# Zero rows for the 64-row products of a hybrid mLSTM, Hyena and neighbourhood-attention trunk

## The chip, the cores and the metric

The kernel runs on one core of one Trainium2 chip. The metric is the device time of one execution in microseconds (us), the median of a few runs. A core has five engines with an instruction queue each: PE (TensorE, matrix products), DVE (VectorE), ACT (ScalarE), POOL (GpSimd) and SP (SyncE, here the issuer of most DMAs). PE multiplies a stationary operand that is loaded into its array first ("PEld" in the profile is that load) with a moving operand that streams through. The array has 128 rows, the contracted dimension, and 128 columns.

## The reference, cut to what matters

Two layers over 1024 latent tokens and 256 context tokens of 1024 channels. The first mixes with an mLSTM and a Hyena long convolution, whose filters come from a small network. The second is a neighbourhood attention of 16 heads of 64 channels; each latent query sees a window of its grid and all context keys. Both layers end in a squared-ReLU MLP.

```python
def hyena_filters(L, w1, b1, w2, b2, w3, freq):
    ...
    h = jnp.sin(freq * (h @ w2 + b2))
    h = (h @ w3).astype(f32).reshape(L, HYENA_ORDER, 2, MIX_B)
    ...
    return h * lax.rsqrt(jnp.sum(h * h, axis=0, keepdims=True) + EPS)

def odd_mixer(hx, hc, w_qkv, qn, kn, rpb, w_out, ctx_out):
    ...
        q = rms_norm(p[:, :, 0], qn) * NA_HD ** -0.5
        k = rms_norm(p[:, :, 1], kn)
    ...
        s_lat = jnp.einsum('bhqd,bhkd->bhqk', q_r, k_blk).astype(f32) + bias.astype(f32)
        s_lat = jnp.where(blk_mask, s_lat, -jnp.inf)
        s_ctx = jnp.einsum('bhqd,bhkd->bhqk', q_r, kc).astype(f32)
        p = jax.nn.softmax(jnp.concatenate([s_lat, s_ctx], axis=-1), axis=-1).astype(v.dtype)
        return (jnp.einsum('bhqk,bhkd->bhqd', p[..., :nk], v_blk)
                + jnp.einsum('bhqk,bhkd->bhqd', p[..., nk:], vc))
```

## The kernel before, in words

Products run in float32r, a float32 whose significand is rounded. To keep accuracy each operand is split into a high part and a low part (the rest after rounding), and a product is the sum hi.hi + hi.lo + lo.hi. Where the contraction has only 64 channels, hi and lo of one operand are stacked on the array's two halves of rows: one product of 128 rows gives hi.hi + hi.lo, and a second one of 64 rows gives lo.hi.

This is done in two stages.

**The filters** (`filter_taps`, early in the program). For each of 8 combinations of channel quarter and order, `w3h` (the high part of the weights, twice, over 128 rows) is multiplied with `h2` (hidden features, hi over lo), then `w3l` (the low part, 64 rows) with the upper half of `h2`: L514 and L515, 6 pairs of products each time, 512 or 256 columns wide. DVE takes the sum out of PSUM, ACT squares it for the norm. Between the pairs on PE stand the products of the filter before (L545 to L549), the transposes of taps (L532) and the sums of the first norm (L253).

**The attention** (`natten_proj`, `natten_attn`). The heads are worked in 8 pairs (`hp`). `natten_proj` computes q, k and v of a pair with `gemm` (L177 to L179), norms q and k (sum of squares by the product L900, then ACT and DVE), and writes q into two tiles Q, one per head hh, with the high part in both halves of the rows (ACT, L930), and the low part into one tile Ql, head 0 in rows 0 to 63, head 1 in rows 64 to 127 (DVE, called from L931, L96 in the profile). The keys go into two tiles KK: k's high part in the head's own half, its low part in the other.

`natten_attn` goes through 4 blocks of columns (cb) and both heads (hh): 8 units a pair of heads, 64 in all. A unit has two row blocks and four pairs of score products: a product with Q over 128 rows (L977), then one with Ql over the 64 rows of its head (L978), 256 columns for the context keys (tile pc) and 384 for the window (tile p_). DVE takes the maximum of the context scores (L981), adds the bias tile TM and takes the maximum of the window scores (L983), ACT forms exponentials (L988, L989), DVE scales them (L993), PE transposes them (L998, L1005), ACT and DVE copy the transposes out (L1000, L1007), and PE multiplies them with the values (L1013, L1017, 64 columns of the array each). The result goes through a tile o to DRAM by a DMA on POOL's queue (L1192). TM is loaded by a DMA on POOL's queue too (L966), and POOL gathers the values' window (L961).

PSUM has 3 banks for scores and results (tag f), 3 for projections (g), one for transposes (m), one for norms (n). A scheduler with priorities sets the order on each engine: the projection of the next pair of heads and the weights' splitting fill the time between the steps of this pair's units. Each engine then works strictly in that order and waits on semaphores.

The functions concerned:

Of the kernel before, what the change touches and what calls it, by code (L numbers as in the profile page):

```python
# [9 lines left out]
F32 = mybir.dt.float32  # L10
F32R = mybir.dt.float32r
# [16 lines left out]
def kernel(ctx: ExitStack, tc: tile.TileContext, A, out):  # L28
# [42 lines left out]
    def psum(**split):  # L71
        """how the eight banks are shared from here on"""
        banks.close()
        psp[:] = [banks.enter_context(tc.tile_pool(name="psp", bufs=1, space=PSUM, reuse_waits="tile")), split]
# [26 lines left out]
    def sub(o, a, b):  # L101
        return tt(o, a, b, ALU.subtract)
# [7 lines left out]
    def split(hi, lo, x, e=None):  # L110
        """x = hi + lo, both rounded to the float32r significand."""
        S.copy(hi, x)  # L112
        (e or V).tensor_tensor(out=lo, in0=x, in1=hi.bitcast(F32), op=ALU.subtract)  # L113

    # ------------------------------------------------------------ constants
# [10 lines left out]
    def rstd_from(ps, n, scale, dst, tmp=None):  # L126
        """dst = (ps * scale + eps) ** -0.5, exp(-0.5 ln v) and one Newton step."""
# [10 lines left out]
    def newton_small(v, dst, tmp):  # L138
        """dst = v ** -0.5 on a small tile."""
# [6 lines left out]
    # ------------------------------------------------------------ weights and products  # L146
# [23 lines left out]
    def gemm(w, h, g, n, M=P, ks=range(8), tag="g"):  # L170
        """out[e, tokens of group g] = sum over the blocks of channels."""
# [25 lines left out]
    # ------------------------------------------------------------ modulation  # L197
# [10 lines left out]
    def mod_steps(l, g, pool, bufs, tag):  # L208
        """2048 columns of the modulation, as 16 steps"""
# [18 lines left out]
    def mod_end(l, g, ps, tag):  # L228
# [9 lines left out]
        # sc1 is blocks 8..15, sc2 blocks 32..39  # L238
# [5 lines left out]
    # ------------------------------------------------------------ norm and modulation of one group of tokens  # L244
    def norm_sum(xk, n, pre, at=None):
        """mean of squares over the channels, in all partitions; xk(k) gives block k"""
# [25 lines left out]
    def norm_group(xk, n, l, sub_i, which, hi, lo, at=None):  # L272
        """xk(k) [P, n] -> hi/lo[:, k, :]"""
# [19 lines left out]
    # ------------------------------------------------------------ MLP  # L293
# [51 lines left out]
    # ------------------------------------------------------------ hyena  # L345
# [10 lines left out]
    def dft_fwd(mm, wp, both=True):  # L356
        """mm(ps, ri, slot) -> X [P, 2, 10, P]"""
# [88 lines left out]
    def sin_reduced(dst, x, pool):  # L446
        """dst = sin(x); x is reduced to [-pi, pi] by a three-part 2 pi."""
# [11 lines left out]
    def filter_hidden(pool, keep):  # L459
        """hidden features, hi over lo; the halves of the positions run in the halves of the partitions"""  # L460
# [37 lines left out]
    def filter_taps(qd, o, h2, dec, fa, fp):  # L498
        """the normed filters of both directions of one channel quarter and order"""
# [3 lines left out]
        w3l = mk(fa, [64, 256], "w3l", 2, F32R)  # L503
# [4 lines left out]
        sub(w3l, w3, w3h[0:64].bitcast(F32))  # L508
        hT = mk(fp, [P, 2, NT], "hT", NHT)
        ss = mk(fp, [P, 4, 2, 3], "ss", 2)  # L510
        for d in range(2):
            for g, (c0, n) in enumerate(GR):
                ps = pt([P, 512], "t")
                T.matmul(ps[:, :n], w3h[:, d * P:(d + 1) * P], h2[:, c0:c0 + n], start=True, stop=False)  # L514
                T.matmul(ps[:, :n], w3l[:, d * P:(d + 1) * P], h2[0:64, c0:c0 + n], start=False, stop=True)  # L515
# [22 lines left out]
    def filter_spectrum(qd, o, hfb, hc, tS, fp, Gd):  # L538
        """spectrum of the two-sided filter -> DRAM"""
# [38 lines left out]
    def hy_block(eb, h, hc, wp):  # L578
        """one block of the projection and its short convolution, [P, 1280]"""
# [29 lines left out]
    def hyena_fft(qd, o, z, hc, wp, Gd):  # L609
        """z (tokens by channels, decimated) -> its product with the filter, ready for the inverse tables"""  # L610
# [16 lines left out]
    def hyena_gate(qd, o, B, X1, x2, hc, wp, mixd):  # L627
        """gate * (filter * z); the last order is left by channels"""
# [24 lines left out]
    # ------------------------------------------------------------ mLSTM  # L653
    def gates(h, mp, keep):
        """gates of all heads as rows 64 d + 10 head + chunk of 128 tokens -> columns, and rows in DRAM to broadcast"""
        with pr("gt"):
            R = 104
            # rows of ps: columns of hi, and of lo 32 below, added up after
# [27 lines left out]
            # lf = min(f, 0) - log1p(exp(-|f|)); log1p(e) = ln(u) + (e - (u - 1)) / u, u = 1 + e  # L686
# [19 lines left out]
            # the running maximum from chunk to chunk: m_prev  # L706
# [49 lines left out]
    def mlstm_head(hd, gs, mp, cst, store):  # L756
        with pr("ms"):
# [36 lines left out]
            # sigmoid(o) = 1 / d, d = 1 + exp(-o): exp(-ln d) and one Newton step  # L794
# [82 lines left out]
    # ------------------------------------------------------------ neighbourhood attention  # L877
# [11 lines left out]
    def natten_proj(hp, h, ap_, nl, cst, order=((0, 0), (0, 1), (1, 0), (1, 1), (1, 2), (2, 0), (2, 1), (2, 2))):  # L889
        """q, k of a pair of heads stacked as hi over lo, and the windows of v"""  # L890
        with pr("np"):
            bd, gain = cst
            # scores = [qhi; qhi] . [khi; klo] + qlo . khi, head hh with khi in its own half
            Q = [mk(nl, [P, LAT], "Q", 4, F32R) for _ in range(2)]
            Ql = mk(nl, [P, LAT], "Ql", 2, F32R)
# [21 lines left out]
            for j, g in order:  # L917
# [5 lines left out]
                if j == 0:  # L923
# [3 lines left out]
                    for hh in range(2):  # L927
# [3 lines left out]
                        sub(blkd(Ql[a, ts]), rv[a], blkd(Q[hh][a, ts]).bitcast(F32))  # L931
# [11 lines left out]
    def natten_attn(hp, qkv, ap_, nl, store):  # L943
        with pr("na"):
# [3 lines left out]
            def tokens(src, n, tag):  # L948
                """channels by tokens -> n blocks of 128 tokens by channels"""
# [8 lines left out]
            for cb in range(4):  # L958
# [5 lines left out]
                for hh in range(2):  # L964
                    TM = mk(nl, [P, 2, 384], "TM", 3)
                    nc.gpsimd.dma_start(TM, A["rpbT"][2 * hp + hh, ct])  # L966
                    a = slice(64 * hh, 64 * hh + 64)
# [4 lines left out]
                    for rb in range(2):  # L972
                        c0 = rb * 512 + cb * P
                        p_ = pt([P, 512], "f")
                        for o, kx in ((pc[:, rb], Kt[hh][:, LAT:NT]),
                                      (p_[:, :384], kl[:, 4 * rb:4 * rb + 12, KC0[cb]:KC0[cb] + 32])):
                            T.matmul(o, Q[hh][:, c0:c0 + P], kx, start=True, stop=False)  # L977
                            T.matmul(o, Ql[a, c0:c0 + P], kx[a], start=False, stop=True)  # L978
# [42 lines left out]
    # ------------------------------------------------------------ layer 0: mixer  # L1021
# [18 lines left out]
    def filler(n, stage):  # L1040
        """n more blocks of q, k, v, o of the heads -> DRAM"""
# [70 lines left out]
    with tc.tile_pool(name="gp", bufs=1, reuse_waits="tile", side="right") as gp:  # L1112
        cst = mlstm_consts(gp)
        with tc.tile_pool(name="ml", bufs=1, reuse_waits="tile") as ml:
# [10 lines left out]
            def out1(d):  # L1125
                """x + gate * product over the first six blocks of the mixer -> DRAM"""
# [56 lines left out]
    # ------------------------------------------------------------ layer 1  # L1183
    with tc.tile_pool(name="nl", bufs=1, reuse_waits="tile") as nl, \
# [3 lines left out]
        def store(hp):  # L1188
            def f(cb, po):
                o = mk(nl, [P, 2, P], "o", 2)  # L1190
# [45 lines left out]
# ---- host side: the inputs laid out for the loads, and constants of the shapes  # L1236
def _layout(I):
    f=lambda a: np.ascontiguousarray(a,dtype=np.float32)
    A={}
    x=np.concatenate([I['x'][0],I['ctx'][0]])          # [1280,1024]  # L1240
# [126 lines left out]
```

## Time and profile before

| | us |
|---|---|
| median of 3 runs (3539.99 to 3546.26) | 3546.22 |
| span of the profiled execution | 3544.9 |
| score products, first to last start (PE) | 2062.0 to 2747.6 |
| w3 products of the filters, first to last start (PE) | 36.3 to 213.9 |
| busy time of POOL | 332.1 |

The span is the time from the first to the last instruction of one execution; the median of the runs stands 1.3 us above it. In the rows of the timeline the shown length of a product includes time in which it is only under way in the array, so what a product costs is the distance from its start to the next one's start. "128*128 128x256" is a product with 128 rows and 128 columns of the array, with a moving operand of 128 partitions and 256 columns; "64*128" has 64 rows. "issue" as the end of an idle time means that nothing which the profile shows was waited for.

### The profile page before, as it was taken

Reading aid. Unit: us, or ns where it says so; the run is one execution under the profiler, and the core shown is the slowest. Engines: PE = TensorE matmul, PEld = TensorE weight load, DVE = VectorE, ACT = ScalarE, POOL = GpSimd, SP = SyncE. Lnnn points to the kernel's source line nnn. Section 1 sums busy time; section 2 is a strip of 40 time slices with the busy share of each in tenths; the row PEclk is TensorE's granted clock in tenths of the full one; section 3 lists DMA queues with packets and bytes.
Section 4 is the critical chain, followed back from the end, with each engine's and each line's share of the span. In section 5 each row is a group of like instructions: output and inputs, shape, how many; then the busy total and the mean of one; then the engine's idle time right before and its main releaser. Section 6 shows DMA issues by size and latency. Waiting matters only on the chain.

```text
span 3544.9 us, 44456 instructions
## 1 busy us (share of the span) xinstructions
PE 3406.1 (96%) x17660; PEld 2676.3 (75%) x17660; DVE 2058.5 (58%) x3655; ACT 1215.0 (34%) x2554; POOL 332.1 (9%) x271
## 2 busy tenths in 40 slices
PE   7889988999989999999999999999999999999999
PEld 3667877677877787787888767777776678888887
DVE  3767979356575444444545875566556665544544
ACT  4643222244343121212121565555555431112211
POOL 0231222101120000000000301111110100000000
PEclk8899999999999999999999999999999999999999
DMA  5331211675632221212110211111113311111111
GB/s 195 133 111 54 85 56 64 230 236 191 209 122 84 75 69 66 77 60 78 48 48 31 79 60 59 60 60 60 60 59 122 106 48 48 48 48 48 48 48 71
DMA packets 104010, 306.06 MB, mean 86 GB/s; under 512 B 12497, under 2 KB 24905, under 8 KB 102394
## 3 DMA queue, kind: packets, MB, share of 16 engines
q1 hardware_dynamic: 94154, 266.60, 22.4%
q0 software_dynamic: 6464, 28.84, 2.6%
q10 hardware_dynamic: 3184, 7.78, 0.7%
q8 instruction: 139, 2.28, 0.3%
q14 instruction: 69, 0.57, 0.0%
HBM read 255.93 MB, written 43.05 MB: 84 GB/s over the span
## 4 chain that ended last, share of the span: by engine, by line
PE 64%; DVE 2%; DMA 2%; ACT 1%; issue 0%; POOL 0%; ACTq 0%; DVEq 0%
PE psg L179 10%; PE psg L177 10%; PE psg L178 10%; PE psf L313 7%; PE psf L314 7%; PE psf L315 7%; PE psf L978 2%; PE psf L977 2%; PE psf L1013 2%; PE psm L218 1%; PE psm L998 1%; PE psn L900 1%; PE psf L1017 1%; DVE n L108 1%; PE psm L1005 1%; DMA wm<-in_w_mod 1%
## 5 line engine op out<-in xcount | busy, mean ns | idle before, releaser
L177 PE MATMUL psg<-h,wh 128*128 128x512 f32 (+1 forms) x2728 | 1020.0, 374 | 17.9 <-ACT wh L112 7.8
L179 PE MATMUL psg<-h,wl 128*128 128x512 f32 (+1 forms) x2728 | 1013.3, 372 | 10.9 <-DVE wl L113 5.9
L178 PE MATMUL psg<-h,wh 128*128 128x512 f32 (+1 forms) x2728 | 1017.5, 373 | 2.4 <-DVE h L108 1.9
L177 PEld LDWEIGHTS psg<-h,wh 128*128 128x128 f32 x2728 | 518.6, 190 | 126.2 <-issue 28.9
L178 PEld LDWEIGHTS psg<-h,wh 128*128 128x128 f32 x2728 | 518.8, 190 | 119.4 <-issue 33.7
L179 PEld LDWEIGHTS psg<-h,wl 128*128 128x128 f32 x2728 | 518.3, 190 | 117.3 <-issue 24.8
L108 DVE SCALAR_TENSOR_TENSOR x<-psf,modT,x 128x512 f32<-128x512 f32 (+1 forms) x512 | 347.2, 683 | 222.6 <-PE psf L315 222.4
L314 PE MATMUL psf<-al,w2h 128*128 128x512 f32 (+1 forms) x1280 | 471.8, 369 | 0.5 <-DVE al L113 0.5
L315 PE MATMUL psf<-ah,w2l 128*128 128x512 f32 (+1 forms) x1280 | 471.3, 368 | 0.0
L313 PE MATMUL psf<-ah,w2h 128*128 128x512 f32 (+1 forms) x1280 | 469.7, 369 | 1.0 <-ACT ah L112 0.8
L112 ACT CAST w2h<-w2r 128x1024 fp32r<-128x1024 f32 x64 | 67.2, 1051 | 762.7 <-PE psf L314 595.9
L313 PEld LDWEIGHTS psf<-ah,w2h 128*128 128x128 f32 x1280 | 240.9, 189 | 45.1 <-ACT ah L112 3.4
L314 PEld LDWEIGHTS psf<-al,w2h 128*128 128x128 f32 x1280 | 241.3, 189 | 42.7 <-DVE al L113 1.8
L315 PEld LDWEIGHTS psf<-ah,w2l 128*128 128x128 f32 x1280 | 241.3, 188 | 41.1 <-issue 1.3
L112 ACT CAST wh<-wr 128x1024 fp32r<-128x1024 f32 (+2 forms) x144 | 148.5, 1031 | 304.0 <-PE psg L178 243.8
L113 DVE TENSOR_TENSOR wl<-wr,wh 128x1024 fp32r<-128x1024 f32 (+1 forms) x105 | 127.7, 1216 | 161.6 <-ACT wh L112 161.6
L108 DVE SCALAR_TENSOR_TENSOR rr<-psg,rr 128x512 f32<-128x512 f32 x160 | 101.4, 634 | 191.7 <-ACT rr L302 191.6
L113 POOL TENSOR_TENSOR wl<-wr,wh 128x1024 fp32r<-128x1024 f32 (+1 forms) x39 | 130.7, 3352 | 622.4 <-ACT wh L112 575.4
L113 DVE TENSOR_TENSOR w2l<-w2r,w2h 128x1024 fp32r<-128x1024 f32 x64 | 78.3, 1223 | 149.2 <-ACT w2h L112 147.5
L302 ACT ACTIVATE rr<-psg 128x512 f32<-128x512 f32 x160 | 88.1, 551 | 213.6 <-PE psg L179 212.3
L112 ACT CAST ah<-rr 128x512 fp32r<-128x512 f32 x160 | 92.4, 578 | 163.6 <-DVE rr L108 163.6
L113 DVE TENSOR_TENSOR al<-rr,ah 128x512 fp32r<-128x512 f32 x160 | 101.8, 636 | 77.6 <-ACT ah L112 77.6
(292 smaller groups left out, 4417.6 us busy)
## 6 DMA issues: line engine op xcount, KB each, us to landing
wm<-in_w_mod SPq DMA_DIRECT2D x96, 512.0 KB
wr<-in_w SPq DMA_DIRECT2D x64, 512.0 KB
w2r<-in_w SPq DMA_DIRECT2D x64, 512.0 KB
big<-d SPq DMA_DIRECT2D x39, 640.0 KB
TM<-in_rpbT POOLq DMA_DIRECT2D x64, 384.0 KB, 3.3
wr<-in_w_in SPq DMA_DIRECT2D x29, 512.0 KB
wr<-in_w_qkv SPq DMA_DIRECT2D x24, 512.0 KB
d<-b SPq DMA_DIRECT2D x8, 1280.0 KB
```

What stands on the lines that cost most here:

```text
L108: return V.scalar_tensor_tensor(out=o, in0=a, scalar=s, in1=b, op0=op0, op1=op1)
L112: S.copy(hi, x)
L113: (e or V).tensor_tensor(out=lo, in0=x, in1=hi.bitcast(F32), op=ALU.subtract)
L177: T.matmul(ps[:M, :n], hi[:, k, :M], hh[g][:, k, :n], start=(i == 0), stop=False)
L178: T.matmul(ps[:M, :n], hi[:, k, :M], hl[g][:, k, :n], start=False, stop=False)
L179: T.matmul(ps[:M, :n], lo[:, k, :M], hh[g][:, k, :n], start=False, stop=(i == len(ks) - 1))
L302: S.activation(r[:, :n], ps[:, :n], AF.Relu)
L313: T.matmul(ps[:, :n], w2h[:, d], ah[g], start=(i == 0), stop=False)
L314: T.matmul(ps[:, :n], w2h[:, d], al[g], start=False, stop=False)
L315: T.matmul(ps[:, :n], w2l[:, d], ah[g], start=False, stop=(i == 1))
L977: T.matmul(o, Q[hh][:, c0:c0 + P], kx, start=True, stop=False)
L978: T.matmul(o, Ql[a, c0:c0 + P], kx[a], start=False, stop=True)
```

## The change

The low parts get as many rows as the array has, with zeros in the added ones. `w3l` becomes 128 rows, with POOL setting rows 64 to 127 to zero before DVE writes the others. Ql becomes one tile per head: the head's low part stands in its own half of the rows, and POOL sets the other half to zero. The products with them (L515, L978; in the changed program L516 and L980) then use all rows of `h2` and KK, and the zeros meet the low parts of the other operand. The memory for it comes from fewer buffers: Ql has 3 of 4 KB per partition for two tiles a pair (before: 2 for one tile), TM 2 of 3 KB in place of 3, o 1 of 1 KB in place of 2.

```diff
         w3h = mk(fa, [P, 256], "w3h", 2, F32R)
-        w3l = mk(fa, [64, 256], "w3l", 2, F32R)
+        w3l = mk(fa, [P, 256], "w3l", 2, F32R)
+        G.memset(w3l[64:128].bitcast(F32), 0.0)
...
-        sub(w3l, w3, w3h[0:64].bitcast(F32))
+        sub(w3l[0:64], w3, w3h[0:64].bitcast(F32))
...
-                T.matmul(ps[:, :n], w3l[:, d * P:(d + 1) * P], h2[0:64, c0:c0 + n], start=False, stop=True)
+                T.matmul(ps[:, :n], w3l[:, d * P:(d + 1) * P], h2[:, c0:c0 + n], start=False, stop=True)
...
-            Ql = mk(nl, [P, LAT], "Ql", 2, F32R)
+            Ql = [mk(nl, [P, LAT], "Ql", 3, F32R) for _ in range(2)]
+            for hh in range(2):
+                G.memset(Ql[hh][64 - 64 * hh:128 - 64 * hh].bitcast(F32), 0.0)
...
-                        sub(blkd(Ql[a, ts]), rv[a], blkd(Q[hh][a, ts]).bitcast(F32))
+                        sub(blkd(Ql[hh][a, ts]), rv[a], blkd(Q[hh][a, ts]).bitcast(F32))
...
-                    TM = mk(nl, [P, 2, 384], "TM", 3)
+                    TM = mk(nl, [P, 2, 384], "TM", 2)
...
-                            T.matmul(o, Ql[a, c0:c0 + P], kx[a], start=False, stop=True)
+                            T.matmul(o, Ql[hh][:, c0:c0 + P], kx, start=False, stop=True)
...
-                o = mk(nl, [P, 2, P], "o", 2)
+                o = mk(nl, [P, 2, P], "o", 1)
```

The rest of the text's difference is comments. Outside the attention the order on PE, DVE and ACT is the same but for single products; POOL has the zeroings between its steps. Three places in the attention show what moves. The names are those of the kernel with a running number behind them; in the changed program every line of `natten_attn` from L969 on stands two lower down than before (L977 is L979), and L900 is L903.

PE, the scores of the last unit of the second pair of heads, before:

```order
L977 MATMUL psf_17260<-KK_16504,Q_16501 128x256
L978 MATMUL psf_17260<-KK_16504,Ql_16502 128x256
L977 MATMUL psf_17262<-KK_16504,Q_16501 128x384
L978 MATMUL psf_17262<-KK_16504,Ql_16502 128x384
L977 MATMUL psf_17260<-KK_16504,Q_16501 128x256
L978 MATMUL psf_17260<-KK_16504,Ql_16502 128x256
L900 MATMUL psn_17462<-n_3105_17460,bd_8236 128x512
L977 MATMUL psf_17268<-KK_16504,Q_16501 128x384
L978 MATMUL psf_17268<-KK_16504,Ql_16502 128x384
```

and the same unit in the changed program:

```order
L979 MATMUL psf_17274<-KK_16518,Q_16512 128x256
L980 MATMUL psf_17274<-KK_16518,Ql_16514 128x256
L979 MATMUL psf_17276<-KK_16518,Q_16512 128x384
L980 MATMUL psf_17276<-KK_16518,Ql_16514 128x384
L979 MATMUL psf_17274<-KK_16518,Q_16512 128x256
L980 MATMUL psf_17274<-KK_16518,Ql_16514 128x256
L903 MATMUL psn_17479<-n_3108_17477,bd_8244 128x512
L177 MATMUL psg_17494<-h_1652_8689,wh_17448 128x512
L178 MATMUL psg_17494<-h_1653_8690,wh_17448 128x512
L979 MATMUL psf_17282<-KK_16518,Q_16512 128x384
L980 MATMUL psf_17282<-KK_16518,Ql_16514 128x384
```

The pairs and the norm product between them keep their places; two projection products have moved up between the last two pairs. The shapes shown are those of the results; the rows of the array are not in them.

DVE, where it writes the low part of q of the third pair of heads, first group of tokens, before:

```order
L96 TENSOR_TENSOR Ql_17331<-n_3095_17371,Q_17329 64x512
L993 TENSOR_SCALAR pe_17013<-pe_17013,st_17007 128x640
L993 TENSOR_SCALAR pe_17019<-pe_17019,st_17007 128x640
L983 ISA pe_17099,st_17087<-psf_17094,TM_17084,st_17087 128x384
L983 ISA st_17087 128x1
L96 TENSOR_TENSOR Ql_17331<-n_3095_17371,Q_17330 64x512
L985 TENSOR_SCALAR st_17087<-st_17087 128x2
```

In the changed program the first head's subtraction stands at the same place, the second head's (into Ql_17346) 32 rows later:

```order
L1009 COPY pc_17190<-psm_17185 128x512
L985 ISA pe_17240,st_17228<-psf_17235,TM_17225,st_17228 128x384
L985 ISA st_17228 128x1
L96 TENSOR_TENSOR Ql_17346<-n_3098_17388,Q_17344 64x512
L987 TENSOR_SCALAR st_17228<-st_17228 128x2
L108 SCALAR_TENSOR_TENSOR n_3103_17432<-psg_17402,gain_8248,n_3103_17432 128x512
```

It has moved to the last block of columns of the second pair, just behind the last scores (psf_17235) of that pair's first head, and ahead of L987 of the same unit.

POOL in the changed program, over the last two blocks of columns of the second pair (zeroings are new, the other steps are those of before with the loads of TM spread out more):

```order
L969 DMA TM_17225<-in_rpbT 128x768
L1194 DMA d_89<-o_17086 256x1x128
L964 COPY vs_17216<-vT_16519 128x512
L969 DMA TM_17272<-in_rpbT 128x768
L898 MEMSET Ql_17346 64x1024
L969 DMA TM_17676<-in_rpbT 128x768
L1194 DMA d_89<-o_17213 256x1x128
L898 MEMSET Ql_18177 64x1024
L969 DMA TM_17723<-in_rpbT 128x768
L1194 DMA d_89<-o_17340 256x1x128
```

Ql_17346 takes the buffer that the second pair's first head still uses, so its zeroing waits for that head's last product with Ql; the loads of TM and the stores of o stand behind it.

More of the change, by code (lines that the diff above doesn't have):

```diff
@@ L964, in natten_attn @@
                 for hh in range(2):
-                    TM = mk(nl, [P, 2, 384], "TM", 3)
+                    TM = mk(nl, [P, 2, 384], "TM", 2)
                     nc.gpsimd.dma_start(TM, A["rpbT"][2 * hp + hh, ct])
-                    a = slice(64 * hh, 64 * hh + 64)
                     kl = Kt[hh][:, 0:LAT].rearrange("p (r c) -> p r c", c=64)
```

## The prediction, made before the changed kernel was run

> **What bounds the kernel now.** I read the page first, for the busy shares and the chain that ended last, then the attention stage by stretches, then who waits for whom there.
>
> ```profile
> PE 3406.1 (96%) x17660; PEld 2676.3 (75%) x17660; DVE 2058.5 (58%) x3655; ACT 1215.0 (34%) x2554; POOL 332.1 (9%) x271
> PE 64%; DVE 2%; DMA 2%; ACT 1%; issue 0%; POOL 0%; ACTq 0%; DVEq 0%
> ```
>
> PE is busy for 96% of the span and nearly all of the chain. The chain's shares add up to 69%, so it is followed back only to about 1100 us: the attention is on it, the filters at the start of the program are not, and for them a stretch has to do. An average over the whole program says little about two small stages, so here are the place of the attention, one stretch inside each stage, and the longest wait of DVE in the attention:
>
> ```profile
> L977 PE MATMUL psf<-KK,Q x256: 276/384/741, 2062.0 to 2747.6; 128*128 128x256 f32 x91, 128*128 128x384 f32 x37
> ...
> core 0: us, PE busy (x) PEld busy (x) DVE busy (x) ACT busy (x) POOL busy (x), PEclk, DMA share, GB/s
> 111.00:122.00 11.00, 11.00 (x66) 8.13 (x65) 10.06 (x21) 7.56 (x18) 2.51 (x3) 1.00 0.55 199
> 2324.00:2411.00 87.00, 86.97 (x514) 61.97 (x513) 52.31 (x115) 51.71 (x129) 9.91 (x16) 1.00 0.19 61
> ...
> DVE st L981 <- PE psf L978: 107.0, 64, 4.1
> ```
>
> The score products run from 2062 to 2748 us. There PE never rests, at the full clock (1.00), while DVE and ACT work 60% of the time, and DVE's first step on each unit (a head and a block of columns, 64 in all) waits 107 us in total for the Ql product. So time taken off PE there comes off the span, until a chain through DVE and ACT becomes the bound. In the filters DVE has 10.06 of 11 us: less room.
>
> But a busy PE is not a PE that computes. The start-to-start distances in the timeline of PE tell what a product really costs (columns: start, shown length, engine, line, operation):
>
> ```profile
> 2357.90 0.28 PE L977 MATMUL psf<-KK,Q 128*128 128x256 f32 x1
> 2358.11 0.38 PE L978 MATMUL psf<-KK,Ql 64*128 64x256 f32 x1
> 2358.42 0.39 PE L977 MATMUL psf<-KK,Q 128*128 128x256 f32 x1
> 2358.65 0.49 PE L998 MATMUL psm<-ident,pe 128*128 128x128 f32 x3
> ...
> 2210.51 0.28 PE L178 MATMUL psg<-h,wh 128*128 128x256 f32 x1
> 2210.63 0.28 PE L179 MATMUL psg<-h,wl 128*128 128x256 f32 x1
> ...
> 2200.47 0.44 PE L978 MATMUL psf<-KK,Ql 64*128 64x384 f32 x1
> 2200.84 0.38 PE L977 MATMUL psf<-KK,Q 128*128 128x256 f32 x1
> ...
> 2203.07 0.50 PE L179 MATMUL psg<-h,wl 128*128 128x512 f32 x1
> 2203.40 0.40 PE L177 MATMUL psg<-h,wh 128*128 128x512 f32 x1
> 2203.64 0.39 PE L178 MATMUL psg<-h,wh 128*128 128x512 f32 x1
> ```
>
> In a stream of full-row products 256 columns take 0.12 us (2210.51 to 2210.63) and 512 take 0.23 (2203.40 to 2203.64). The same 256 columns take 0.21 when the next product has 64 rows (2357.90), 0.23 when the one before had 64 rows (2358.42), and 0.31 for the 64-row product between two others (2358.11). So a change of shape costs about 0.09 us before it and 0.10 to 0.11 after it. The second part shows again at 2203.07: the first full product after an Ql product takes 0.33 in place of 0.23. The weight loads say why:
>
> ```profile
> 2203.06 0.19 PEld L179 LDWEIGHTS psg<-h,wl 128*128 128x128 f32 x1 [0.19 <-issue]
> 2203.17 0.19 PEld L177 LDWEIGHTS psg<-h,wh 128*128 128x128 f32 x1
> 2203.41 0.19 PEld L178 LDWEIGHTS psg<-h,wh 128*128 128x128 f32 x1
> ```
>
> In the stream a load starts a whole product ahead (2203.41 for the product of 2203.64). After the change of shape the load of L179 starts only with its product (2203.06 and 2203.07), after an idle 0.19: its time is not hidden, and before it the array seems to empty, 0.09. The price of a change is 0.19 us. 384 columns fit: 0.37 from 2200.47 to 2200.84, where a value between 0.12 and 0.23 would be 0.175.
>
> **The change, part by part.** How often this is paid:
>
> ```profile
> L978 PE MATMUL psf<-KK,Ql 64*128 64x384 f32 x128 | 57.1, 446 | 0.0
> L978 PE MATMUL psf<-KK,Ql 64*128 64x256 f32 x128 | 48.9, 382 | 0.0
> L515 PE MATMUL pst<-h2s,w3l 64*128 64x512 f32 x32 | 17.7, 553 | 0.0
> L515 PE MATMUL pst<-h2s,w3l 64*128 64x256 f32 x16 | 6.7, 420 | 0.0
> ...
> 111.20 0.47 PE L514 MATMUL pst<-h2s,w3h 128*128 128x512 f32 x1
> 111.61 0.50 PE L515 MATMUL pst<-h2s,w3l 64*128 64x512 f32 x1
> 112.03 0.49 PE L545 MATMUL psf<-hfb,tF 128*128 128x128 f32 x2
> ```
>
> 256 Ql products and 48 w3l products, hardly ever two in a row, make two changes each. Along PE's order 598 changes fall away: 506 in the attention (a few edges stay, where a score product meets the 64-column products L1013 and L1017) and 92 in the filters. The changes to and from 64 and 32 columns stay. The same number of products and columns is left, and a full-row product of the same width costs no more than its columns, as the stream shows. Gross: 506 x 0.193 = 97.7 us, and 92 x 0.19 = 17.5 us (L515 takes 0.42 at 111.61, 0.19 over 0.23).
>
> What of it is kept? Unit 27 of the attention, with the rows that gate PE:
>
> ```profile
> 2345.31 0.69 DVE L981 TENSOR_REDUCE st<-psf 128x2 f32<-128x512 f32 x1 [4.07 <-PE psf L978]
> 2347.45 1.01 DVE L993 TENSOR_SCALAR pe<-pe,st 128x640 f32<-128x640 f32 x2
> 2348.38 0.17 DVE L985 TENSOR_SCALAR st<-st 128x2 f32<-128x2 f32 x1
> ...
> 2348.54 0.49 PE L998 MATMUL psm<-ident,pe 128*128 128x128 f32 x3
> 2350.03 0.49 PE L998 MATMUL psm<-ident,pe 128*128 128x128 f32 x3
> ...
> 2348.59 0.62 ACT L988 ACTIVATE pe<-pe,st 128x384 f32<-128x384 f32 x1
> 2349.20 0.46 ACT L1000 COPY s<-psm 128x384 f32<-128x384 f32 x1
> ```
>
> The transposes L998 at 2348.54 need the first half of L993, done at about 2347.95: 0.6 us of slack. A unit has four pairs of score products, 8 changes, 1.54 us, so PE would wait 1 us per unit if DVE stood still. It doesn't: it had idled 4.07 us for PE's L978 when it began at 2345.31, and its steps follow PE forward. Where they don't follow quite: the second transposes (2350.03) need the one bank of tag m back, copied out by L1000, which stands on ACT behind L988, which waits for DVE's L985; slack 2350.03 - 2349.66 = 0.37. Moving these rows forward by hand I get a wait of about 0.25 us in every second unit: 64 x 0.13 = 8 us, an estimate.
>
> The zeroing of Ql is new on POOL. Two rows of its kind, and the load whose buffers shrink:
>
> ```profile
> masks.py:197 POOL MEMSET ident<- 128x128 f32 x1 | 0.2, 205 | 0.3 <-POOLq L1359 0.3
> L1359 POOL MEMSET const-float32-1.0<- 128x1 f32 x1 | 0.1, 104 | 0.0
> ...
> TM<-in_rpbT POOLq DMA_DIRECT2D x64, 384.0 KB, 3.3
> ```
>
> 104 ns for one column and 205 for 128 make 0.8 ns a column: about 0.9 us for 1024 (1.6 if it is all in proportion), an estimate. 16 of them are 15 us on an engine that is 9% busy. Their price is a wait. With three buffers for two tiles a pair, the second head's Ql lies where the running pair's first head has its own, so its zeroing waits for that head's last scores; behind it DVE's subtraction into that Ql waits, and behind that in DVE's order L985 (now L987) of the same unit, its exponentials, and the r tile, one of four n2 buffers, that the next K norm needs. The zeroing runs while DVE does that unit's last 0.6 us step, so DVE loses about 0.3 us, plus 0.69 for a subtraction that now stands ahead of L985. For 7 pairs between 0 and 11 us; I take 6. Queued behind the zeroing on POOL are the next TM loads and stores of o, which have time: a TM is needed two units (some 20 us) after its buffer is free, and takes 0.6 to issue and 3.3 to land; the single o is needed once per block of columns, again some 20 us apart. I cost both at nothing; if that cover failed, it would be 3 us in some unit. The eight zeroings of w3l, 64x256, are 0.3 us each on an idle POOL, their buffers two filters old: nothing. ACT, SP and the stages after attention keep their work.
>
> Attention: 97.7 - 8 - 6 = 84. Filters: bounds are 0 and 17.5; since DVE is nearly full beside PE there, I keep 60%, 10.5. Together 94. The profiled execution has 3544.9, which becomes 3451; the median of the runs shown is 1.3 above its span, so **3452 us**.
>
> **Rivals.** (1) The chain through DVE and ACT takes over. For: slack is only 0.37 to 0.6 us per unit against 1.54 saved; if DVE stood still, 0.6 of 1.54 would be kept, 38 + 6 us, 3502. Against: DVE's 107 us of waiting for L978. With half kept, 49 + 9: 3488. (2) A load into rows that the running product uses is not hidden, so full-row pairs pay 0.10 for each load and save only the emptying: 598 x 0.09 = 54, 3492 before any wait. Against: the load at 2203.41 lies whole under the product of 2203.40. [...] (3) Slower: the late second Ql holds back the next pair's K norms, and with them its first scores, past the products that fill. The chain of waits shows one group of K in the first pair, from its square to its last step:
>
> ```profile
> 2048.44 0.61 ACT n L898
> ...
> 2059.38 0.70 DVE KK L96
> ```
>
> 11.6 us with other steps between. If one group lay bare in each of 7 pairs, 81 us would go, 3533; two groups make 163, 3615. It decides from 94 / 7 = 13.5 us a pair. Against: PE's new order has those scores in the old place, with 30 and more projection products behind them to fill.
>
> (4) The zero rows change nothing, because what costs is the change of operands and not of rows: 3546 to 3552. Against: the 2203.40 stream changes operands each time.
>
> **How the numbers follow.** Forecast 0.70, with its own range 3430 to 3475; more than gross 0.03; rival 1 0.15; 2 0.05; 4 0.03; 3 0.04. Low end: all 115 us kept, 3431, rounded to 3428; the high end takes in rival 1 at half and the lower edge of 2, 3492. Faster by over 0.2% (7 us, about what a measurement of this kernel tells from no change) 0.93, within 0.03, slower 0.04.
>
> **What would show it.** Right: L980 (before L978) with 128 rows, 0.12 and about 0.175 us to the next start, no "issue" idle before its load; the stretch from the first score product to the last in some 600 us where it has 686; DVE's wait for the scores smaller. Wrong: distances still 0.31 and 0.37 (rival 4), 0.22 and 0.28 (rival 2); PE idle before L1000, L979 or L1015 of over 5 us per pair, released by DVE or ACT (rival 1); idle PE with DVE waiting on POOL's zeroing (rival 3).

## The result and the profile after

The changed kernel takes **3438.66 us** (median of 4 runs, 3435.15 to 3440.34), the kernel before beside it 3543.65 us (4 runs, 3539.99 to 3546.26): a ratio of **0.9706**, 95% interval 0.9692 to 0.9719. That is 105.0 us less; 94 had been forecast, and the time is 13 us below the 3452 on record. The profiled execution spans 3438.5 us.

The page of the changed kernel: busy time and share of each engine, then the shares of the chain that ended last.

```profile
PE 3288.0 (96%) x17660; PEld 2647.1 (77%) x17660; DVE 2055.2 (60%) x3655; ACT 1209.4 (35%) x2554; POOL 350.3 (10%) x295
PE 76%; DVE 12%; DMA 5%; ACT 3%; POOL 3%; issue 2%; SPq 0%; ACTq 0%; DVEq 0%; POOLq 0%
```

PE has as many products as before and 118 us less busy time (3406.1 before). It still bounds the kernel; DVE and ACT are within 6 us of before, and POOL has 18 us more, its zeroings.

The timeline of PE and of the weight loads, in a unit of the attention (start, shown length, engine, line, operation; L979 and L980 are L977 and L978 of before):

```profile
2185.82 0.34 PE L979 MATMUL psf<-KK,Q 128*128 128x384 f32 x1
2186.00 0.34 PE L980 MATMUL psf<-KK,Ql 128*128 128x384 f32 x1
2186.18 0.28 PE L979 MATMUL psf<-KK,Q 128*128 128x256 f32 x1
2186.29 0.28 PE L980 MATMUL psf<-KK,Ql 128*128 128x256 f32 x1
2186.41 0.34 PE L979 MATMUL psf<-KK,Q 128*128 128x384 f32 x1
...
2186.18 0.19 PEld L980 LDWEIGHTS psf<-KK,Ql 128*128 128x128 f32 x1
2186.30 0.19 PEld L979 LDWEIGHTS psf<-KK,Q 128*128 128x128 f32 x1
```

From 2186.00 to 2186.18 a Ql product of 384 columns takes 0.18 (0.37 before), from 2186.29 to 2186.41 one of 256 takes 0.12 (0.31 before). The load for the product of 2186.29 starts at 2186.18, with the product ahead of it. The whole stage, and the filters, by stretches (us, then the busy time of each engine, the granted clock, the DMA share and GB/s), first of the changed kernel and then of the kernel before:

```profile
30.00:250.00 220.00, 182.68 (x1124) 144.09 (x1123) 147.83 (x315) 136.90 (x302) 67.51 (x63) 0.94 0.42 144
2037.00:2641.00 604.00, 593.13 (x3965) 464.94 (x3963) 419.24 (x954) 395.67 (x998) 87.39 (x133) 0.99 0.25 77
```

```profile
30.00:250.00 220.00, 188.52 (x1005) 137.78 (x1006) 145.95 (x308) 128.85 (x286) 55.77 (x49) 0.86 0.39 133
2061.00:2748.00 687.00, 683.70 (x3966) 484.31 (x3965) 419.71 (x954) 399.73 (x999) 75.68 (x119) 0.99 0.21 68
```

In the attention the same work of DVE and ACT (419 and 396 us) stands in 604 us where it had 687, and PE's idle time there has grown from 3.3 us (687 - 683.70) to 10.9. In the filters the granted clock is 0.94 where the profile of before had 0.86. That was not foreseen, and it is what the experiments have to settle.

The place of the changed kernel's score products and of its w3 products, with their first and last start:

```profile
L979 PE MATMUL psf<-KK,Q x256: 274/342/582, 2037.7 to 2640.9; 128*128 128x256 f32 x92, 128*128 128x384 f32 x36
L516 PE MATMUL pst<-h2s,w3l x48: 277/393/430, 39.4 to 190.0; 128*128 128x512 f32 x32, 128*128 128x256 f32 x16
```

And its waits in the attention (us in total, times, longest):

```profile
DVE st L983 <- PE psf L980: 62.3, 40, 2.8
PE psm L1000 <- ACT s L1002: 4.2, 11, 0.8
PE psm L1000 <- DVE pe L995: 2.1, 7, 0.6
...
PE psf L979 <- DVE KK L96: 0.2, 1, 0.2
```

From first to last score product: 603.2 us, 82.4 less than before. DVE's wait for the Ql product has shrunk from 107.0 to 62.3 us, so it still mostly waits for PE, and PE waits for it and for ACT only now and then, at the transposes L1000. Ahead of the attention 24 us have gone too, in the filters; behind it nothing has changed (797.3 us from the last score product to the end before, 797.6 after).

### The profile page after: what moved, and what is told of

Same layout as the page of the kernel before. It is cut to its first block, busy times and chain, and to the rows that moved or that the text cites. A ratio compares the mean times of both kernels' runs of the same rounds, so it can differ in the third digit from the quotient of the medians.

```text
span 3438.5 us, 44541 instructions
## 1 busy us (share of the span) xinstructions
PE 3288.0 (96%) x17660; PEld 2647.1 (77%) x17660; DVE 2055.2 (60%) x3655; ACT 1209.4 (35%) x2554; POOL 350.3 (10%) x295
## 4 chain that ended last, share of the span: by engine, by line
PE 76%; DVE 12%; DMA 5%; ACT 3%; POOL 3%; issue 2%; SPq 0%; ACTq 0%; DVEq 0%; POOLq 0%
PE psg L178 12%; PE psg L179 12%; PE psg L177 12%; PE psf L313 7%; PE psf L314 7%; PE psf L315 7%; DMA wm<-in_w_mod 2%; DVE b L96 2%; PE psf L1015 2%; DVE n L108 2%; PE psm L1000 1%; DVE q L96 1%; PE psm L218 1%; PE psf L979 1%; PE psf L980 1%
## 5 line engine op out<-in xcount | busy, mean ns | idle before, releaser
L178 PE MATMUL psg<-h,wh 128*128 128x512 f32 (+1 forms) x2728 | 1017.1, 373 | 4.1 <-DVE h L108 2.8
L178 PEld LDWEIGHTS psg<-h,wh 128*128 128x128 f32 x2728 | 519.7, 191 | 120.6 <-issue 33.8
```

Of the source, the lines that this page charges most:

```text
L178: T.matmul(ps[:M, :n], hi[:, k, :M], hl[g][:, k, :n], start=False, stop=False)
```

## The experiments

Two questions: is it the change of shape that cost the time, and not another part of the edit; and why did the filters give 24 us in the profile, more than the 17.5 that the prediction had as their most? The comparisons with before are with the runs of the kernel before on the same chip.

**The filter part alone.**

```diff
-        w3l = mk(fa, [64, 256], "w3l", 2, F32R)
+        w3l = mk(fa, [P, 256], "w3l", 2, F32R)
+        G.memset(w3l[64:128].bitcast(F32), 0.0)
...
-                T.matmul(..., h2[0:64, c0:c0 + n], start=False, stop=True)
+                T.matmul(..., h2[:, c0:c0 + n], start=False, stop=True)
```

> The kernel before with the filter part of the change alone: w3l with 128 rows, the lower half of the rows zeroed by POOL, its product over all rows. Theory A (a change between 64 and 128 rows costs about 0.19 us, 92 of them fall away, and what goes beyond that in the profile of the changed kernel came from a higher granted clock by chance): 10 to 17.5 us less, ratio 0.995 to 0.997, and in the stretch from 30 to 250 us the granted clock is 0.86 as in the profile of before. Theory B (the gain is 25 us because PE, less interrupted in the filters, also gets a higher clock): 22 to 26 us less, ratio 0.9927 to 0.9938, granted clock 0.94 in that stretch. The attention takes 685 to 687 us from its first to its last score product by either.

Measured: 3525.68 us against 3541.42, ratio 0.9946 (0.9929 to 0.9963). In its profile the filters' stretch looks as in the changed kernel:

```profile
30.00:250.00 220.00, 181.75 (x1121) 143.31 (x1120) 148.77 (x315) 136.73 (x303) 66.56 (x63) 0.94 0.41 142
```

By its interval that is 13 to 25 us: nearer to theory A in time, with theory B in the clock of its one profile. So this run alone doesn't decide; the clock of one execution is only that of one execution. The attention shows the same. Its code is that of before, and 685 to 687 us were expected, but in this profile it takes 696:

```profile
2033.50:2729.40 695.90, 692.59 (x3961) 489.96 (x3961) 418.20 (x953) 398.95 (x996) 75.49 (x119) 0.98 0.21 67
```

PE works as before; the trace's clock records have three stretches of half clock between 2198 and 2486 us, 24 us together, that the profile of before doesn't have. So the lengths of a stage in two profiles tell two programs apart only where the clocks agree.

**The attention part alone**, with the fewer buffers, filters as before.

> The kernel before with the attention part alone: one Ql tile per head with zeros in the other half of the rows, and the fewer buffers for TM and o; the filters as before. By the theory that 506 changes of shape at 0.193 us fall away and some 15 us of that are lost in waits: 80 to 84 us less, about 3461 us, and the distance from the first to the last score product 603 us. If the filters' shorter time had helped the attention or the other way round, the two parts would not add up to the 105 us of the whole change: then 70 or 95. Granted clock from 30 to 250 us: 0.86 if it belongs to the filters' old products, anything if it is chance.

Measured: 3446.24 us against 3541.42, ratio 0.9722 (0.9699 to 0.9745), so 95 less. The place of its first product of each pair of scores (L978 in this kernel):

```profile
L978 PE MATMUL psf<-KK,Q x256: 274/342/582, 2048.7 to 2652.1; 128*128 128x256 f32 x92, 128*128 128x384 f32 x36
```

and its filters' stretch:

```profile
30.00:250.00 220.00, 189.80 (x1045) 139.48 (x1046) 147.58 (x310) 132.87 (x292) 61.70 (x56) 0.91 0.41 142
```

The stage is 603.4 us long, as expected, but the time fell by 11 us more than the 80 to 84 expected. By the medians alone this would be the outcome "95", in which the two parts don't add up: 16 and 95 are more than 105. The clocks decide that below. The old filters have a clock of 0.91 here and 0.86 in the profile of before: the clock of this stage differs from execution to execution of the same code.

**64 rows kept, the order changed.** In each row block the two Q products come first, then the two Ql products.

```diff
-                        for o, kx in (...):
+                        for o, kx in two:
                             T.matmul(o, Q[hh][:, c0:c0 + P], kx, start=True, stop=False)
+                        for o, kx in two:
                             T.matmul(o, Ql[a, c0:c0 + P], kx[a], start=False, stop=True)
```

> The kernel before with all products, tiles and rows as they were, but in another order: in each row block the two Q products first, then the two Ql products of 64 rows. Half of the 506 changes between 64 and 128 rows in the attention go, nothing else. Theory A (the change of shape is what costs, 0.19 us a time): 49 us less gross, 35 to 45 kept, 3499 to 3509 us; the first of two neighbouring Ql products is 0.12 us (256 columns) from the second less the 0.09 for emptying, that is it still pays on its own edge, and the second pays no load. Rival (a product of 64 rows is itself slow, whatever stands beside it): within 5 us of before. Rival (a weight load into rows that the running product uses can't be hidden): little gain as well, since two Ql products of one head use the same rows.

Measured: 3524.55 us against 3541.42, ratio 0.9945 (0.9922 to 0.9968); 674.7 us from the first to the last score product (685.6 before). The expectation had the number of changes wrong: the scheduler took most of the groups apart again. In the trace only 26 of 128 row blocks have their two Ql products side by side, and 459 changes of rows are left of 511. The 52 that went are worth 52 x 0.193 = 10 us, and the stage is 10.9 shorter, at the same clock (0.99) as before. Where the group held, its timeline prices both edges of a product apart (here L978 is Q and L980 Ql; "x2" is two products in one row, 0.23 apart for Q and 0.22 for Ql):

```profile
2202.70 0.56 PE L978 MATMUL psf<-KK,Q 128*128 128x256 f32 x2
2203.20 0.56 PE L980 MATMUL psf<-KK,Ql 64*128 64x256 f32 x2
2203.69 0.50 PE L178 MATMUL psg<-h,wh 128*128 128x512 f32 x1
...
2202.70 0.30 PEld L978 LDWEIGHTS psf<-KK,Q 128*128 128x128 f32 x2 [0.20 <-issue]
2203.19 0.29 PEld L980 LDWEIGHTS psf<-KK,Ql 64*128 64x128 f32 x2 [0.20 <-issue]
```

Q and Ql of 256 and 384 columns take 0.50 and 0.49 us together (2202.70 to 2203.20 to 2203.69), where their columns are worth 0.12 + 0.175 = 0.295: each group of two pays 0.20, once, whatever its rows. By the trace's starts the first product of a group pays 0.10 (median of 26: 0.223 for a 256-column Ql with another shape ahead of it and the same behind it), the last pays 0.09 (0.268 for a 384-column Ql with the same shape ahead of it and another behind), and a Ql product with other shapes on both sides pays both (0.310 and 0.372). The changed kernel's trace shows the same edges on products of 128 rows: where the 64-column products stand next to a Ql product, it takes 0.223 for 256 columns (6 of them, another shape ahead) and 0.273 for 384 (8, another shape behind). A product of 64 rows is not slow in itself: both rivals of this experiment fall.

**Fewer buffers alone**: TM 2 in place of 3, o 1 in place of 2, all else as before.

> The kernel before with only two buffers for TM in place of three and one for o in place of two; products, Ql and rows as before. Prediction's step: costs nothing, within 3 us (ratio 0.9992 to 1.0008). Rival (part of the 15 us lost in the attention is a TM load or a store of o that comes late): 3 to 10 us more, with DVE's window step waiting for the TM load, or ACT's copy into o for the store before.

Measured: 3539.46 us against 3541.42, ratio 0.9991 (0.9976 to 1.0005); the attention's stretch 687.2 us (685.6). They cost nothing that can be seen, and in the trace DVE has no wait for a TM load, nor ACT one for a store of o.

**The changed kernel again, and the clock.**

> The changed kernel itself, more often, beside runs of the kernel before on the same chip. The two parts alone, taken at equal clock, gave 12 and 84 us of gain, 96 together; the medians differ by 105. Theory A (the 10 us between are a granted clock that happened to be low in the runs of before): with more runs the mean clocks of the two kernels come together, 0.982 to 0.983 each, and the ratio goes to 0.9730. Theory B (the changed kernel is throttled less): mean clock 0.985 against 0.982 again, ratio 0.970 to 0.971.

> The changed kernel beside the two others, for the comparison on the same chip: 3434 to 3442 us, 603 us from the first to the last score product, and a mean clock of 0.984 to 0.986 against 0.982 to 0.984 for the kernel before if it is throttled less, the same clock if not.

Measured: 3436.84 against 3535.97 us (0.9717, 0.9704 to 0.9731) on the one chip, 3433.02 against 3540.95 (0.9702, 0.9680 to 0.9723) on the other; the stretch of scores 603.1 and 600.9 us. On the first chip the ratio lies between the two theories, and the mean clocks are 0.985 and 0.984; on the second they are 0.986 and 0.983. Each run gives its mean granted clock; only all runs together decide:

| | runs | mean us | mean clock | us at a clock of 0.983 |
|---|---|---|---|---|
| before (beside the experiments) | 42 | 3539.2 | 0.9825 | 3538.0 |
| filter part alone | 6 | 3525.0 | 0.9833 | 3525.9 |
| grouped, 64 rows | 5 | 3523.4 | 0.9840 | 3526.1 |
| fewer buffers | 12 | 3538.9 | 0.9827 | 3538.2 |
| attention part alone | 4 | 3447.3 | 0.9852 | 3453.5 |
| changed | 13 | 3436.1 | 0.9854 | 3442.7 |

The last column moves each run along a line fitted through the 42 runs of before, whose time falls by 27.7 us for each 0.01 of clock; the line explains 64% of their variance. At equal clock the filter part is worth 12.1 us, the attention part 84.5, together 96.6, and the whole change 95.3, so the parts add up. The other 8 of the 103 us between the means go with the clock, which is higher by 0.0029 in the changed kernel (standard errors 0.0003 and 0.0004). So theory B holds over all runs: the changed kernel is throttled less, by little.

The filters by themselves say the same. From the first w3 product to the same later product of PE (the 1076th) the four profiles with the old filters take 218.8, 209.9, 209.7 and 205.7 us at clocks of 0.87, 0.93, 0.92 and 0.96 of that stretch; those of the changed kernel and of the filter part alone 192.1, 193.5, 200.6 and 197.1 at 0.95, 0.95, 0.91 and 0.93. At 0.92 to 0.93 that is 209.8 against 197.1, 13 us. A line through all thirteen profiles, with the clock of this stretch and the kind of filters as its two terms, gives 13.4 us (standard error 0.6). The profile of before had the lowest clock of all, and the 9 us by which it lies above 209.8 stood in the first comparison.

**Ql zeroed once.** Before the loop over the pairs, fixed tiles are set to zero; in the loop there is no zeroing. First with one tile for head 1 and two for head 0, then the other way round (diff against the changed kernel; the tiles QL are made ahead of the loop):

```diff
-            Ql = [mk(nl, [P, LAT], "Ql", 3, F32R) for _ in range(2)]
-            for hh in range(2):
-                G.memset(Ql[hh][64 - 64 * hh:128 - 64 * hh].bitcast(F32), 0.0)
+            Ql = [QL[0][hp % 2], QL[1][hp % 1]]
```

> The changed kernel, but the zeros are written once ahead of the loop and not for each pair: head 0 has two tiles of its own for Ql, head 1 one. No zeroing stands in the loop, but the low part of head 1 must wait until the running pair's head 1 has had its last scores, one unit later than in the changed kernel. Theory A (lateness of the second Ql is what costs, the zeroing is hidden): 3 to 10 us more than the changed kernel, with DVE's subtraction waiting longer for the score products. Theory B (the zeroing in the loop costs, 7 times about 0.95 us): 0 to 5 us less. If neither lies on the path: within 3 us.

> The changed kernel, zeros written once ahead of the loop: head 0 has one tile for Ql, head 1 two. The low part waits for the last scores of the running pair's head 0 as in the changed kernel, without the zeroing between. Theory A (lateness): within 2 us of the changed kernel. Theory B (the zeroing in the loop costs 7 times about 0.95 us): 4 to 7 us less. The prediction took 6 us for both together.

> The kernel whose zeros are written once, head 0 with one tile for Ql and head 1 with two, more often. If taking the zeroing out of the loop is a real gain: 3 to 6 us less than the changed kernel on the same chip, and the stretch from the first to the last score product 599 us against 603. If the first difference was noise: within 2 us, and 603 us.

Measured: with one tile for head 1 3440.13 us, ratio to before 0.9728 (0.9713 to 0.9742), 604.6 us for the stretch of scores; with one tile for head 0 3432.44 us, 0.9708 (0.9694 to 0.9721), and again 3430.48 us, 0.9693 (0.9673 to 0.9714), with 599.0 and 598.9 us for the stretch. The changed kernel on the same two chips: 3436.84 and 3433.02 us, 603.1 and 600.9 (the 600.9 at a clock of 1.00, the others at 0.99). In the trace of the changed kernel the zeroing and, with one tile for head 1, DVE's subtraction wait for the score products:

```profile
L898 POOL MEMSET Ql<- 64x1024 f32 x16 | 15.2, 948 | 67.4 <-PE psf L980 67.3
```

```profile
DVE Ql L96 <- PE psf L979: 6.2, 7, 2.3
```

With one tile for head 0 neither wait is there. PE's waits at the transposes, 6.3 us in the changed kernel (4.2 + 2.1), are 2.6 us in it (its L999 is the changed kernel's L1000):

```profile
PE psm L999 <- ACT s L1001: 2.1, 4, 0.7
PE psm L999 <- DVE pe L994: 0.5, 2, 0.3
```

This version is the fastest of all, by 4.2 us in the mean of 9 runs against 13 of the changed kernel (3431.9 against 3436.1), 5.3 at equal clock. On the one chip it came out as theory B had it (4.4 us less), on the other between the two outcomes (2.5 less; 3 to 6 or at most 2 had been expected), with the 599 us of a real gain in both profiles. How the 5 us come about is not shown. In the changed kernel POOL waits 67 us for the score products, but no row has DVE or PE waiting for the zeroing; what moves with the edit is the order of DVE's steps. The version with one tile for head 1 saves the zeroing as well and gains nothing: its median is 3.3 us above the changed kernel, which is not clear of noise, and its stretch of scores is 5.6 us longer than with one tile for head 0. So the subtraction one unit later may well cost that much, but order and wait are not told apart.

**Another bank for the second transposes.** The bank of tag m, which the prediction blamed for 8 us, gets relief: the second transposes of a unit go to tag g (projections), or to tag n (norms).

```diff
-    TA, TB, TC, TV, PO = "m", "m", "m", "m", "f"
+    TA, TB, TC, TV, PO = "m", "g", "m", "m", "f"
```

> The changed kernel, with the second transposes of the window's weights of each unit in a bank of the projections (tag g) in place of the one bank of tag m. Theory A (the 8 us booked for waits behind the transposes come from that one bank, given back by ACT's copy): the waits of the transposes for ACT's copy (4.2 us on PE, 19.9 us of the weight loads) mostly go, 3 to 8 us less than the changed kernel. Rival (ACT and DVE are late anyway, and the wait only moves to the next transposes, or the projections miss the bank): within 2 us or more than the changed kernel, with waits of the projection products for a bank of tag g.

> The changed kernel, with the second transposes of the window's weights in the bank of the norms (tag n), which the projections don't use. In PE's order the projection products stay spread over the units of a pair (30, 4, 14, 2, 5, 2, 5, 2 groups of three) but for the first pair, whose last four units get none. Theory A (the transposes' waits for ACT's copy come from the one bank of tag m): these waits go, 3 to 8 us less in pairs 2 to 8, and some 5 us more in the first pair, together -3 to +2. Theory B (ACT and DVE are late themselves): the wait moves to DVE's scaling of the weights, 0 to 5 us more in pairs 2 to 8, 5 to 10 us more together.

Measured: 3640.68 us with g, ratio to before 1.0288 (1.0271 to 1.0305); 3526.2 us with n, 0.9960 (0.9943 to 0.9977): 204 and 93 us more than the changed kernel on the same chip, far beyond what any theory had put a number to. The stretch of scores, with g and then with n:

```profile
2034.60:2819.70 785.10, 670.64 (x3922) 510.52 (x3922) 418.79 (x944) 400.50 (x994) 84.59 (x133) 0.90 0.18 58
2033.20:2728.50 695.30, 627.66 (x3964) 482.11 (x3964) 425.81 (x951) 401.13 (x996) 85.16 (x133) 0.96 0.21 67
```

With g, two neighbouring stretches of the attention: the first two rows have all work (busy time and count of PE, PEld, DVE, ACT and POOL, then the granted clock, the DMA share and GB/s), the other two the projection products L178 alone (PE and PEld):

```profile
2254.00:2310.00 56.00, 45.11 (x283) 33.47 (x285) 25.42 (x68) 22.61 (x69) 8.26 (x13) 0.73 0.17 56
2310.00:2374.00 64.00, 57.80 (x318) 45.05 (x315) 35.48 (x71) 35.06 (x76) 5.62 (x9) 1.00 0.15 48
...
2254.00:2310.00 56.00, 0.80 (x1) 0.29 (x1) 0.73 0.17 56
2310.00:2374.00 64.00, 24.16 (x63) 11.88 (x63) 1.00 0.15 48
```

The scheduler now puts 63 of the L178 products into one stretch and 1 into another (56 and 50 in the changed kernel in the same stretches). Without them the chain through DVE and ACT lies bare: PE is idle 11 of 56 us, and its clock falls to 0.73. Of the 182 us by which the stage is longer, the clock of 0.90 in place of 0.99 is worth at most 0.09 x 785 = 71, an estimate. With n the order changes too. PE now waits for DVE's scaling of the weights at the transposes, for the last steps of the norms ahead of projections, and for ACT's squares ahead of the norm products L903:

```profile
PE psm L1000 <- DVE pe L995: 19.2, 16, 3.0
PE psg L177 <- DVE n L96: 14.5, 7, 2.1
PE psn L903 <- ACT n L901: 13.2, 19, 1.2
```

The wait of L1000 for L1002 is gone there, and dearer ones stand in its place. Whether the one bank cost the changed kernel anything could not be tried without such side effects, and stays open, and no row names the bank of tag n as what is waited for. Shown is that with this scheduler a bank taken from g or n costs far more than 8 us.

## Why the prediction was right, and where it was off

- **PE bounds, and the change of shape is the price**: right. The distances went from 0.31 and 0.37 to 0.12 and 0.18, and the third experiment showed the two parts, 0.10 on the first product behind a change and 0.09 on the last ahead of one, with the rows kept. Where the 0.10 is paid, the loads of a group start only with its first product (2203.19 and 2203.20), after an idle 0.20, so its load isn't hidden. That the array empties ahead of a change, as the prediction read the other 0.09, was not shown; the rows give the time alone.
- **Attention, 97.7 gross, 84 kept**: 82.4 in the profile and 84.5 at equal clock, but its parts were each too large, and that the two errors cancel is luck. PE's idle time grew by 7.6 us, not by 14; so the changes were worth 82.4 + 7.6 = 90 us, 0.178 each over 506, not 0.193. By the distances from start to start without idle time, 82 of the 90 lie on the score products and 7 on the projection products beside them; why the average is below the 0.19 of the products shown isn't settled.
- **8 us behind the transposes**: the waits of L1000 for ACT and DVE are 6.3 us (4.2 + 2.1), and 1.1 of them stood there before. **6 us for the second Ql**: some 5, by the version without the zeroing in the loop. The size is near, the way is not: the prediction had DVE wait behind the zeroing, and the trace has no such wait. Nor do the two add up, since that version takes away 3.7 of the 6.3 us.
- **Filters, 10.5 of 17.5 kept**: 12.1 by the part alone and 13 by the stages at like clock. The share of 60% was chosen and not worked out, and what takes the other 4 to 5 us isn't shown. Of the 24 us in the first comparison of profiles some 13 are the change, and most of the rest is the low clock in the profile of before.
- **Fewer buffers, zeroing of w3l, POOL's time**: nothing, as booked. A zeroing of 64x1024 took 948 ns where 0.9 us was estimated, of 64x256 307 ns where 0.3 was.
- **The rivals.** (1) DVE and ACT as the bound: DVE still waits 62.3 us for the Ql product, and PE for the transposes in 18 places only. The slack was small for a DVE that stands still, and DVE followed. With the projections bunched the bare chain and the lower clock there (0.90 in the stage) cost 204 us. (2) Loads not hidden: the load at 2186.18 lies beside the product of 2186.18, rows 0 to 127 both, and the distances are 0.12 and 0.18, not 0.22 and 0.28. (3) K norms held back: PE waits once, 0.2 us, for a KK tile. (4) Zero rows change nothing: 82 us.

The step that was off is one that the prediction didn't write as a term: it subtracted 94 us from the span of **one** execution and took the granted clock to stay as it was. At equal clock the sum is 95.3 against 94. The clock is worth 8 us in the means of all runs, and the median from which the prediction started, 3546.22, was 7 us above the mean of 42 other runs (3539.2). These 1, 8 and 7 us, less 3 by which the first four runs of the changed kernel lie above the mean of 13, are the 13 us between 3452 and 3438.66. Why the clock is higher is shown only in kind (below); in which stage the changed kernel is throttled less stays open, since the profiles differ among themselves in every stage.

## What to carry to other kernels

On a matrix engine that is busy all the time, look at the distances from start to start where neighbours have different shapes: here rows filled with zeros cost no time on PE (0.12 us for 256 columns, as in the stream of full-row products) and saved 0.18 us for each change of shape; 82 of 90 us were left after the waits, since nothing else became the bound. Before a bank or a buffer is moved to relieve a wait of a few us, ask what the scheduler will do with the work that fills the gaps: here the move cost 204 and 93 us, and the wait had been booked at 8. And where a granted clock is shown, compare it stage by stage before a difference of two profiles is explained by the code.

## What the runs showed of the hardware that was not expected

In the traces of the kernels before and after, the granted clock is 1.00 or 0.50 and nothing between. They have 43 records at 0.50: 18 of 3.41 us, 15 of 6.83, 7 of 10.24, one of 17.07, and two that the end of the trace breaks off. The clock records of the thirteen profiles, cut into windows of 3.41 us, the shortest whole record, give for the windows at full clock (from 20 us to the end; idle by PE's shown lengths):

| idle share of PE in a window at full clock | windows | share of them with the next one at half clock |
|---|---|---|
| under 0.05 | 11308 | 0.00 (4 of them) |
| 0.05 to 0.40 | 961 | 0.00 (4 of them) |
| 0.40 to 0.50 | 151 | 0.19 |
| 0.50 to 0.70 | 156 | 0.78 |
| over 0.70 | 126 | 1.00 |

So in these profiles waiting in pieces was mostly enough: 0.78 of the windows that were idle for 0.50 to 0.70 had one at half clock behind them. In the kernel with the second transposes in g the window ahead of a halving was idle for 0.64 of its time, with a longest piece of 1.9 us (medians of 39), and 11 us of idle time in 56 came with a clock of 0.73. In the filters single windows come that far, though PE is busy for 188.52 of 220 us in the profile of before: ahead of its eight halvings from 30 to 250 us it was idle for 0.26 to 0.86 of the window, and the clocks of that stretch lie between 0.86 and 0.95 over the profiles. Idle time doesn't account for all: four halvings follow windows in which PE was busy all but 2% of the time, three of them in the attention of the filter part alone, and what brought them on stays open.
